# A hybrid decoder layer on one core: another order and engine choice for the first stage, loads by single blocks, five weight places in turn

## The chip, the core and the metric

The kernel is one program on one core of a Trainium2 chip. The metric is the time of one execution on the device in microseconds (us), less being better. Three runs of the kernel before took 858.31, 863.84 and 863.96 us; their median is 863.84 us.

## The reference

One layer on x of 512 tokens by 1024 channels, all in float32:

```python
h = x @ w_in[l]                                     # one projection feeds everything
y_a = nsa_attention(nsa_q, cmp_k, ..., nsa_gate) @ w_nsa_out[l]      # 8 heads of 64, 3 branches
y_b = gated_deltanet(gdn_qkv, beta, decay, gate) @ w_gdn_out[l]      # 4 heads of 128, chunks of 64
mix = (sigmoid(gate_a) * y_a + sigmoid(gate_b) * y_b) @ w_o[l]
x = layer_norm(ALPHA * x + mix, ln1_g[l], ln1_b[l])
f = conv_ffn(x, ffn_w_up[l], ffn_conv_w[l], ffn_w_down[l])           # 1024 -> 2 x 2816 -> 1024
x = layer_norm(ALPHA * x + f, ln2_g[l], ln2_b[l])
```

In each DeltaNet head a unit lower triangular system of 64 by 64 is solved in each chunk (`solve_triangular(eye + m, eye)`); the attention has a compressed, a selected and a window branch.

## The kernel before

**Products.** Every float32 product is made of three products of rounded halves: a = hi + lo, and hi·hi + lo·hi + hi·lo are added up in PSUM. So each weight block is loaded (`raw`), rounded by ACT (`wh`, L216) and its rest taken by DVE or POOL (`wl`, L220, or L1043 in the last stage), before TensorE (PE) can use it. `split_w` does this in the first stage; which engine takes a step is looked up in the table `ENGINE` (A, V and G are ACT, DVE and POOL), with names such as `ws13` for the `wl` of unit 13, `wh13` for its `wh`, and `sq1` for the last step of q in head 1.

**Stages** (times of the profiled execution): a start in which the token-major columns are made for all tokens at once (`token_major`, L270 to L292, tiles `pb`; 5 to 19 us); the first stage up to 366 us, in which the projection's other columns are made unit by unit (`gemm_t`, tiles `gps`, L230 to L233), the four DeltaNet heads are worked off and the attention's blocks of scores are made (L777, L778), normalised, transposed (L806) and multiplied with the values (L823); the merge and the output projection until 500 us; the FFN's first product (tiles `pu`) until 741 us; the FFN's second product (L1107) until 852 us; the last normalisation.

**What sets the order.** In the first stage each step has a short name: q0 is the convolution of head 0, n0 the triangular solve of head 0 (`gdn_tri`, L490 to L564), o0 its output, a0 to a7 and b0 to b7 the attention's heads, and so on. `ORDER` lists the steps, `SHIFT` moves one in the planner's eyes by some units of time, and a scheduler that is given the priorities writes out one order of instructions for each engine. Each engine then works its own list strictly in that order, and waits at an instruction until its inputs are there. DMAs of inputs are issued from SyncE's (SP's) list in the same manner, and a tile's place in a pool (`BUFS` gives how many) has to come free before it is loaded again.

**The triangular solve.** For head h, POOL or DVE makes `lo` (L494) and `gx` (L502), PE spreads them (L504), ACT copies them (L505), and DVE works off 30 small steps in a row, `tmp = lx * xs` (L511) and `xs = xs + tmp` (L512). The result is spread to `z` (L514), and only then PE can transpose it (L402, `dps<-ident,z`) and go on in short dependent products.

**The FFN's second product.** It is made as seven products of half matrices (`go`, L1121). `go` works through groups of two weight blocks (`block`, L1027 to L1045); the first of a group takes one of three places (`wh`, `wl`), the second one of two (`wh2`, `wl2`). The two halves of the tokens (t = 0 and 1) have a PSUM bank each (`px`, `pz`, `pu`). After the last group of a product DVE takes the banks into x (L1137, L1141). The sums of activations for later products are split in between (`sum_parts`, hs on ACT, sl on DVE, L1102).

Of the kernel before, what the change touches and what calls it, by code (L numbers as in the profile page):

```python
# [2 lines left out]

# [125 lines left out]


@with_exitstack
def body(ctx: ExitStack, tc: tile.TileContext, d, out):
# [136 lines left out]

    def token_major():  # L270
        pss = [pb.tile([128, 288], F32, name=f"pb{t}") for t in range(TT)]
        for k0 in range(0, KD, 2):
            load_x(k0)
            hi, lo = split_w(d["wB"][:, k0:k0 + 2, :], [128, 2, 288], V)
            load_x(k0 + 1)
            for i in range(2):
# [2 lines left out]
                for t in range(TT):
                    ts = slice(t * 128, (t + 1) * 128)  # L280
                    PE.matmul(pss[t], xh[:, k, ts], wh, start=(k == 0), stop=False)
                    PE.matmul(pss[t], xh[:, k, ts], wl, start=False, stop=False)
                    PE.matmul(pss[t], xl[:, k, ts], wh, start=False, stop=(k == KD - 1))
# [936 lines left out]
```

## Time and profile before

| what | value |
|---|---|
| runs, median | 863.84 us (858.31 to 863.96) |
| the profiled execution, its span | 861.92 us, 860.1 us |
| PE busy | 832.0 us (97%), 4226 matmuls |
| DVE busy | 598.1 us (70%) |
| ACT busy | 404.9 us (47%) |
| POOL busy | 171.2 us (20%) |
| DMA | 108.05 MB, 126 GB/s in the mean |

An engine's busy time is the sum of the time in which it had an instruction under way. For PE this says less than it seems: matmuls are pipelined, and one that runs at half the clock is as busy as one at the full clock. So the places where PE waits, and the clock it was granted, have to be read beside it.

### The profile page before, as it was taken

Reading aid. Unit: us, or ns where it says so; the run is one execution under the profiler, and the core shown is the slowest. Engines: PE = TensorE matmul, PEld = TensorE weight load, DVE = VectorE, ACT = ScalarE, POOL = GpSimd, SP = SyncE. Lnnn points to the kernel's source line nnn. Section 1 sums busy time; section 2 is a strip of 40 time slices with the busy share of each in tenths; the row PEclk is TensorE's granted clock in tenths of the full one; section 3 lists DMA queues with packets and bytes.
Section 4 is the critical chain, followed back from the end, with each engine's and each line's share of the span. In section 5 each row is a group of like instructions: output and inputs, shape, how many; then the busy total and the mean of one; then the engine's idle time right before and its main releaser. Section 6 shows DMA issues by size and latency. Waiting matters only on the chain.

```text
span 860.1 us, 11841 instructions
## 1 busy us (share of the span) xinstructions
PE 832.0 (97%) x4226; PEld 685.1 (80%) x4226; DVE 598.1 (70%) x1257; ACT 404.9 (47%) x891; POOL 171.2 (20%) x160
## 2 busy tenths in 40 slices
PE   9999799999899999999999999999999999999996
PEld 8777687778777778888888898888888888887774
DVE  5666479976656876484557637777777777867686
ACT  5553277476356766542234104444444444654541
POOL 0423531414425311202100002111111111100000
PEclk9999799999999999999999999999999999999999
DMA  8323111002011100254347006998875832565562
GB/s 263 109 73 123 37 39 50 26 25 72 27 50 50 41 34 25 74 172 147 123 147 245 24 2 224 277 243 270 189 230 155 221 95 76 173 208 178 180 230 98
DMA packets 35051, 108.05 MB, mean 126 GB/s; under 512 B 3632, under 2 KB 4016, under 8 KB 34608
## 3 DMA queue, kind: packets, MB, share of 16 engines
q1 hardware_dynamic: 27696, 84.23, 30.3%
q0 software_dynamic: 7296, 23.07, 11.3%
q8 instruction: 33, 0.54, 0.3%
q14 instruction: 26, 0.21, 0.1%
HBM read 105.19 MB, written 25.17 MB: 152 GB/s over the span
## 4 chain that ended last, share of the span: by engine, by line
PE 53%; DVE 6%; DMA 5%; issue 1%; ACT 1%; POOL 1%; DVEq 0%; ACTq 0%; POOLq 0%
PE pu L232 9%; PE pu L230 9%; PE pu L233 9%; PE gps L232 3%; PE gps L233 3%; PE gps L230 3%; DMA raw<-wsum 3%; DVE wl L1043 2%; DMA raw<-in_down 2%; PE pw L986 2%; PE pw L984 2%; PE pm L230 2%; PE pw L985 2%; PE pm L232 2%; PE pm L233 2%
## 5 line engine op out<-in xcount | busy, mean ns | idle before, releaser
L220 DVE TENSOR_TENSOR wl<-raw,wh 128x512 fp32r<-128x512 f32 (+1 forms) x142 | 112.2, 791 | 79.7 <-ACT wh L216 66.3
L216 ACT ACTIVATE wh<-raw 128x512 fp32r<-128x512 f32 (+1 forms) x152 | 93.7, 620 | 146.9 <-PE pu L232 100.8
L230 PE MATMUL pu<-mh,wh 128*128 128x512 f32 (+1 forms) x384 | 142.7, 372 | 0.0
L232 PE MATMUL pu<-ml,wh 128*128 128x512 f32 (+1 forms) x384 | 142.6, 371 | 0.0
L233 PE MATMUL pu<-mh,wl 128*128 128x512 f32 (+1 forms) x384 | 142.6, 371 | 0.0
L230 PE MATMUL gps<-xh,wh 128*128 128x512 f32 x320 | 128.9, 404 | 1.4 <-DVE tmp L511 0.8
L232 PE MATMUL gps<-xl,wh 128*128 128x512 f32 x320 | 128.6, 402 | 0.0
L233 PE MATMUL gps<-xh,wl 128*128 128x512 f32 x320 | 128.4, 402 | 0.0
L230 PEld LDWEIGHTS pu<-mh,wh 128*128 128x128 f32 x384 | 72.4, 188 | 12.6
L233 PEld LDWEIGHTS pu<-mh,wl 128*128 128x128 f32 x384 | 72.4, 188 | 12.4
L232 PEld LDWEIGHTS pu<-ml,wh 128*128 128x128 f32 x384 | 72.4, 188 | 12.4
L220 POOL TENSOR_TENSOR wl<-raw,wh 128x512 fp32r<-128x512 f32 x42 | 55.5, 1323 | 134.0 <-ACT wh L216 59.0
L1065 DVE SCALAR_TENSOR_TENSOR fa<-pu,fcw,fa 128x511 f32<-128x511 f32 x88 | 65.7, 746 | 10.8 <-ACT fa L1062 9.2
L230 PEld LDWEIGHTS gps<-xh,wh 128*128 128x128 f32 x320 | 60.6, 190 | 12.8 <-issue 2.2
L232 PEld LDWEIGHTS gps<-xl,wh 128*128 128x128 f32 x320 | 60.6, 190 | 11.3 <-issue 0.7
L233 PEld LDWEIGHTS gps<-xh,wl 128*128 128x128 f32 x320 | 60.6, 190 | 10.5
L1071 POOL TENSOR_TENSOR fth<-fth,fa 128x512 f32<-128x512 f32 x22 | 28.7, 1304 | 201.5 <-DVE fa L1065 201.5
L1042 ACT ACTIVATE wh<-raw 128x512 fp32r<-128x512 f32 x67 | 39.6, 625 | 44.1 <-DMA raw<-wsum 17.5
L1043 DVE TENSOR_TENSOR wl<-raw,wh 128x512 fp32r<-128x512 f32 x67 | 44.9, 701 | 21.9 <-ACT wh L1042 21.7
L263 POOL TENSOR_TENSOR rs<-rs,minus_half 128x1 f32<-128x1 f32 x8 | 7.6, 946 | 184.1 <-DVE rs L945 184.1
L783 ACT ACTIVATE sc<-sc,mn 128x384 f32<-128x384 f32 (+2 forms) x64 | 35.8, 560 | 15.6 <-DVE mn L781 14.9
L1062 ACT ACTIVATE fa<-pu,fcw 128x512 f32<-128x512 f32 x44 | 29.6, 672 | 10.2 <-PE pu L233 10.2
(328 smaller groups left out, 1685.4 us busy)
## 6 DMA issues: line engine op xcount, KB each, us to landing
raw<-in_up SPq DMA_DIRECT2D x44, 512.0 KB, 4.8
raw<-in_wT SPq DMA_DIRECT2D x40, 512.0 KB, 3.5
wsum<-in_down POOLq DMA_DIRECT2D x6, 2816.0 KB, 24.4
raw<-wsum SPq DMA_DIRECT2D x20, 512.0 KB, 4.3
raw<-in_down SPq DMA_DIRECT2D x15, 512.0 KB, 4.0
wsum<-wsum POOLq DMA_DIRECT2D x2, 2816.0 KB, 12.2
raw<-in_wm SPq DMA_DIRECT2D x8, 512.0 KB, 3.7
raw<-in_wo SPq DMA_DIRECT2D x8, 512.0 KB, 3.8
```

The lines of the kernel that those rows point to most:

```text
L216: A.activation(wh, r, AF.Copy)
L220: eng.tensor_tensor(wl, r, wh.bitcast(F32), op=OP.subtract)
L230: i = PE.matmul(ps, wh[k], mh_(k), start=(k == 0), stop=False)
L232: PE.matmul(ps, wh[k], ml_(k), start=False, stop=False)
L233: PE.matmul(ps, wl[k], mh_(k), start=False, stop=(k == n - 1))
L783: A.activation(s[:, i, :n], s[:, i, :n], AF.Exp, scale=-1.0, bias=mn[:, 0, i:i + 1], accum_out=mn[:, 1, i:i + 1])
L984: PE.matmul(ps, mh[:, k, ts], woh[:, k, cs], start=(k == 0), stop=False)
L1042: A.activation(hi, raw[:, i], AF.Copy)
L1043: V.tensor_tensor(lo, raw[:, i], hi.bitcast(F32), op=OP.subtract)
L1062: A.activation(acc, ps, AF.Copy, scale=w[:, 2:3])
L1065: V.scalar_tensor_tensor(acc[:, n:], ps[:, :S - n], w[:, i:i + 1], acc[:, n:], op0=OP.mult, op1=OP.add)
L1071: G.tensor_tensor(th, th, g[1], op=OP.mult)
```

## The change

It has four parts, none of which changes what is computed.

1. Other tables `ORDER`, `SHIFT` and `ENGINE`, so that the first stage's steps stand in another order and some of them on other engines.
2. `load_x` becomes `load_block(k)`: x and the token-major weights `wB` are loaded one block k at a time (before: wB in pairs of blocks); x's first two blocks come in two halves of tokens; the `wh` of block 0 is made by DVE.
3. The pool `mid` has 3 places where it had 4, `out` 4 where it had 3.
4. In the FFN's second product the five places are taken in turn by the blocks, whichever group they are in, and a group works block by block (both token halves of a block, then the next block). Only the last group of a product that has `then` works token half by token half, as all did before.

PE issues the same matmuls in number and form. Over the whole program DVE issues 10 more `wl` of 128x512 (201 to 211), 3 more casts, 2 more steps `kq` and `vraw`, one more tap of the convolution, 2 more `gx` of 128x256, one more `z`, 5 more steps L791, one `lo` less and 3 fewer steps L794 (29 to 26); POOL 10 fewer `wl` (42 to 32), 2 fewer `th` and 2 fewer `kq` or `vraw`, one fewer tap, `gx` 2 fewer, one fewer `z`, one more `lo`, 8 more casts (12 to 20). SP issues 8 loads of wB where it issued 4, and 10 of x where it issued 8.

```diff
@@ tables (SHIFT and ENGINE are left out)
...
-ORDER = "q0 k0 i0 q1 j0 m0 c n0 i1 p0 j1 v0 v1 o0 a0 b0 y0 a1 m1 n1 i2 j2 b1 a2 o1 b2 y1 m2 v2 q2 a3 n2 b3 o2 y2 q3 g0 p1 k1 a4 i3 b4 j3 m3 a5 n3 b5 g1 v3 a6 g2 b6 o3 a7 g3 g4 b7 g5 y3".split()
+ORDER = "q0 k0 i0 q1 j0 m0 c n0 i1 j1 v0 v1 p0 o0 a0 b0 y0 a1 m1 b1 a2 n1 i2 j2 b2 o1 y1 m2 v2 a3 n2 q2 b3 o2 y2 q3 g0 p1 k1 i3 j3 a4 b4 m3 a5 n3 g1 g2 b5 a6 v3 g3 b6 a7 g4 b7 o3 g5 y3".split()
...
-BUFS = {"w2": 2, 'in': 3, 'st': 6, 'mid': 4, 'out': 3, 'att': 4, 'ob': 1, 'qf': 2, 'kq': 2, 'lx': 1, 'pg': 2, 'pd': 2, 'pa': 3, 'raw': 3, 'wh': 3, 'wl': 3, 'q2': 4, 'mg': 6, 'mr': 4}
+BUFS = {"w2": 2, 'in': 3, 'st': 6, 'mid': 3, 'out': 4, 'att': 4, 'ob': 1, 'qf': 2, 'kq': 2, 'lx': 1, 'pg': 2, 'pd': 2, 'pa': 3, 'raw': 3, 'wh': 3, 'wl': 3, 'q2': 4, 'mg': 6, 'mr': 4}
@@ the token-major start
-    def load_x(k):
+    def load_block(k):
+
         xr = slot("mid", "xr")
-        nc.sync.dma_start(out=xr, in_=d["xT"][:, k, :])
-        A.activation(xh[:, k, :], xr, AF.Copy)
-        V.tensor_tensor(xl[:, k, :], xr, xh[:, k, :].bitcast(F32), op=OP.subtract)
+        raw = wp.tile([128, 288], F32, name="raw", bufs=BUFS["raw"])
+        wh = wp.tile([128, 288], F32R, name="wh", bufs=BUFS["wh"])
+        wl = wp.tile([128, 288], F32R, name="wl", bufs=BUFS["wl"])
+        n = 2 if k < 2 else 1
+        halves = [slice(i * S // n, (i + 1) * S // n) for i in range(n)]
+        for i, ts in enumerate(halves):
+            nc.sync.dma_start(out=xr[:, ts], in_=d["xT"][:, k, ts])
+            if i == 0:
+                nc.sync.dma_start(out=raw, in_=d["wB"][:, k, :])
+            A.activation(xh[:, k, ts], xr[:, ts], AF.Copy)
+            if i == 0:
+                if k == 0:
+                    V.tensor_copy(wh, raw)
+                else:
+                    A.activation(wh, raw, AF.Copy)
+                V.tensor_tensor(wl, raw, wh.bitcast(F32), op=OP.subtract)
+            V.tensor_tensor(xl[:, k, ts], xr[:, ts], xh[:, k, ts].bitcast(F32), op=OP.subtract)
+        return wh, wl
...
-        for k0 in range(0, KD, 2):
-            load_x(k0)
-            hi, lo = split_w(d["wB"][:, k0:k0 + 2, :], [128, 2, 288], V)
-            load_x(k0 + 1)
-            for i in range(2):
-                k = k0 + i
-                wh, wl = hi[i], lo[i]
...
+        for k in range(KD):
+            wh, wl = load_block(k)
...
@@ the FFN's second product
+    turn = itertools.cycle(range(5))
...
-            elif i:
+            elif next(turn) > 2:
                 hi = fp.tile([128, S], F32R, name="wh2", bufs=BUFS["w2"])
                 lo = fp.tile([128, S], F32R, name="wl2", bufs=BUFS["w2"])
...
-            for t in range(2):
-                for j, w in zip(js, ws):
-                    three(ps[t], a, j, t, w, fresh and j == 0, j == NP - 1)
+            pairs = [(j, w, t) for j, w in zip(js, ws) for t in range(2)]
+            if then is not None and g == len(GROUPS) - 1:
+                pairs.sort(key=lambda x: x[2])
+            for j, w, t in pairs:
+                three(ps[t], a, j, t, w, fresh and j == 0, j == NP - 1)
```

**The start, SP's list.** Rows are line, DMA, tile and shape. Before, the first weight block of the first stage (`wT`) is issued ahead of the constants:

```order
L202 DMA xr<-in_xT 128x512
L209 DMA raw<-in_wT 128x1024
L302 DMA cst<-in_consts 128x1444
L305 DMA ident<-in_consts 128x128
L312 DMA gcw<-in_gcw 128x48
```

Now, behind the constants:

```order
L210 DMA xr<-in_xT 128x512
L314 DMA cst<-in_consts 128x1444
L226 DMA raw<-in_wT 128x1024
L317 DMA ident<-in_consts 128x128
L324 DMA gcw<-in_gcw 128x48
```

The 722 KB of constants now stand ahead of the first `wT`. On PE the first products of the first stage (`gps`), which stood between the last token-major ones, now all come after them.

**Head 0's solve, POOL's list** while DVE works off the 30 steps. Before (`th` and `kq` are the last steps of head 1's q):

```order
L220 TENSOR_TENSOR wl_1171<-raw_1167,wh_1169 128x512
L220 TENSOR_TENSOR wl_1175<-raw_1167,wh_1173 128x512
L395 TENSOR_TENSOR th_1091<-th_1091,acc_1086 128x512
L396 TENSOR_TENSOR kq_950<-th_1091,acc_1086 128x4x128
L507 COPY xs_2330<-cst_305 128x64
```

Now:

```order
L237 TENSOR_TENSOR wl_1096<-raw_1088,wh_1094 128x512
L237 TENSOR_TENSOR wl_1148<-raw_1144,wh_1146 128x512
L237 TENSOR_TENSOR wl_1152<-raw_1144,wh_1150 128x512
L519 COPY xs_2298<-cst_319 128x64
L237 TENSOR_TENSOR wl_1409<-raw_1405,wh_1407 128x512
```

The two steps are one step of DVE now, and stand there behind `z`. PE's products between L504 and the transposes of `z` are 49 of 128x512 before and now.

**Head 2's solve, PE's list** up to the transposes of `z`. `cs` is the compressed branch's probabilities. Before:

```order
L232 MATMUL gps_2747<-xl_94,wh_2743 128x512
L233 MATMUL gps_2747<-xh_93,wl_2745 128x512
L402 MATMUL aps_2728<-ident_307,cs_2713 128x128 x4
L402 MATMUL dps_2365<-ident_307,z_2363 128x128 x4
L523 MATMUL dps_2372<-z_2363,m_2131 128x64 x4
```

Now:

```order
L250 MATMUL gps_2584<-xh_93,wl_2582 128x512
L247 MATMUL gps_2584<-xh_93,wh_2580 128x512
L414 MATMUL dps_2333<-ident_321,z_2331 128x128 x4
L535 MATMUL dps_2340<-z_2331,m_2144 128x64 x4
L414 MATMUL aps_2742<-ident_321,cs_2727 128x128
```

The transposes of `cs` moved behind those of `z`, and between L504 and `z` there are 46 products of 128x512 where there were 37.

## Rows read from the trace of the kernel before

**Rows 1.** The page: the engines' busy us, share of the span, instructions.

```profile
PE 832.0 (97%) x4226; PEld 685.1 (80%) x4226; DVE 598.1 (70%) x1257; ACT 404.9 (47%) x891; POOL 171.2 (20%) x160
```

**Rows 2.** Windows: length, busy PE, PEld, DVE, ACT, POOL, clock, DMA share, GB/s.

```profile
140.00:179.00 39.00, 36.99 (x198) 28.65 (x196) 37.55 (x120) 22.01 (x56) 12.46 (x12) 1.00 0.13 41
...
283.00:305.00 22.00, 20.48 (x110) 15.71 (x109) 20.66 (x72) 15.24 (x38) 4.41 (x5) 1.00 0.13 44
...
740.00:860.00 120.00, 109.05 (x468) 86.40 (x466) 89.16 (x140) 55.03 (x89) 5.40 (x5) 0.98 0.56 182
```

**Rows 3.** The same view of shorter windows.

```profile
80.00:100.00 20.00, 15.62 (x65) 13.03 (x64) 13.84 (x35) 5.37 (x9) 9.16 (x8) 0.79 0.18 53
...
175.00:200.00 25.00, 24.02 (x176) 19.70 (x175) 18.61 (x67) 20.66 (x68) 5.97 (x7) 0.93 0.06 15
225.00:250.00 25.00, 22.38 (x150) 18.32 (x149) 17.95 (x51) 11.90 (x28) 6.65 (x7) 0.93 0.15 44
```

**Rows 4.** PE's waits: who waited for whom, us in total, times, longest.

```profile
PE dps L402 <- DVE z L514: 3.6, 1, 3.6
PE aps L402 <- DVE xs L512: 1.7, 1, 1.7
PE px L1107 <- DVE wl L1043: 1.5, 2, 1.0
...
PE pz L1107 <- DVE wl L1043: 0.9, 2, 0.7
...
PE pb L281 <- ACT wh L216: 0.5, 1, 0.5
```

**Rows 5.** Timeline of DVE in head 0's solve: start, duration, instruction.

```profile
80.91 0.21 DVE L512 TENSOR_TENSOR xs<-xs,tmp 128x52 f32<-128x52 f32 x1
81.16 1.21 DVE L511 TENSOR_TENSOR tmp<-lx,xs 128x48 f32<-128x48 f32 x1
...
90.17 1.14 DVE L512 TENSOR_TENSOR xs<-xs,tmp 128x8 f32<-128x8 f32 x1
```

**Rows 6.** Timeline of POOL beside it.

```profile
81.00 1.30 POOL L220 TENSOR_TENSOR wl<-raw,wh 128x512 fp32r<-128x512 f32 x1 [4.23 <-ACT wh L216]
...
90.02 1.27 POOL L395 TENSOR_TENSOR th<-th,acc 128x512 f32<-128x512 f32 x1 [2.28 <-ACT th L391]
91.36 1.27 POOL L396 TENSOR_TENSOR kq<-th,acc 128x512 f32<-128x512 f32 x1
```

**Rows 7.** Timeline of PE behind head 0's solve.

```profile
93.44 1.12 PE L402 MATMUL dps<-ident,z 128*128 128x128 f32 x4 [3.60 <-DVE z L514]
...
96.48 0.63 PE L233 MATMUL gps<-xh,wl 128*128 128x512 f32 x1
...
102.21 0.40 PE L233 MATMUL gps<-xh,wl 128*128 128x512 f32 x1
102.45 0.40 PE L230 MATMUL gps<-xh,wh 128*128 128x512 f32 x1
```

**Rows 8.** Groups by line up to 366 us: busy us, mean ns.

```profile
L220 POOL TENSOR_TENSOR wl<-raw,wh 128x512 fp32r<-128x512 f32 x38 | 49.3, 1299 | 92.3 <-ACT wh L216 59.0 <-DVE wh L218 13.2 <-PE gps L233 11.3
...
L220 DVE TENSOR_TENSOR wl<-raw,wh 128x512 fp32r<-128x512 f32 x27 | 19.1, 706 | 18.3 <-POOL wh L218 8.8 <-ACT wh L216 7.3 <-PE aps L692 1.6
```

**Rows 9.** DMAs issued before 16 us: KB each, median us to landing.

```profile
raw<-in_wT SPq DMA_DIRECT2D x2, 512.0 KB, 6.6
cst<-in_consts SPq DMA_DIRECT2D x1, 722.0 KB, 7.9
```

**Rows 10.** Timeline of SP and of PE in the start.

```profile
11.06 0.42 SPq L302 DMA_DIRECT2D cst<-in_consts  x1
...
18.13 0.39 PE L230 MATMUL gps<-xh,wh 128*128 128x512 f32 x1
```

**Rows 11.** Timeline of PE and DVE where a weight block comes late.

```profile
806.15 2.35 DVE L1102 TENSOR_TENSOR sl<-sr,hs 128x1024 fp32r<-128x1024 f32 x2
...
809.16 0.50 PE L1107 MATMUL pz<-wl,hs 128*128 128x512 f32 x1 [0.70 <-DVE wl L1043]
```

More of the change, by code (lines that the diff above doesn't have):

```diff
@@ L1 @@
+import itertools
 import math
@@ L123 @@
 LAG = 1
-SHIFT = {'q0': -80, 'a0': -2606, 'b0': -1465, 'a1': -346, 'b1': -377, 'a2': -230, 'q3': -2244, 'j3': -430, 'a4': -1433, 'g2': 1384, 'o2': -123, 'i1': -141, 'b5': -1403, 'y2': 203, 'q1': -513, 'g1': -578, 'y3': 2104, 'y1': -290, 'b3': -285, 'k0': -80, 'm2': 160, 'g3': 1052, 'b6': 744, 'v2': 140, 'j1': -94, 'm0': 33, 'b7': -911, 'o3': -214, 'y0': 12, 'q2': -38, 'g4': 84, 'm3': -270, 'v0': -40, 'j0': -160, 'v1': -14, 'o1': -84, 'v3': -40, 'o0': 67, 'n2': -1041, 'g0': -210, 'b2': -127, 'k1': -309, 'j2': 199, 'p0': 131, 'a3': -41, 'm1': -225, 'n3': -4, 'n1': -883, 'i0': 12, 'a5': -2, 'p1': -12, 'i2': -88, 'i3': -21, 'n0': -6, 'a6': 155}
@@ L125 @@
-ENGINE = {'p16': 'A', 'p55': 'V', 'p24': 'G', 'p32': 'A', 'vb0': 'A', 'p43': 'A', 'p04': 'G', 'p54': 'A', 'p20': 'G', 'kd2': 'A', 'p25': 'A', 'kd0': 'V', 'p06': 'A', 'vb1': 'A', 'lo3': 'G', 'p44': 'A', 'p45': 'G', 'p34': 'G', 'p36': 'A', 'kd1': 'A', 'kd3': 'A', 'sq1': 'G', 'xs3': 'G', 'vb2': 'A', 'wh31': 'V', 'ws4': 'G', 'ws11': 'V', 'ws29': 'G', 'p03': 'A', 'wh2': 'A', 'wh43': 'G', 'p37': 'A', 'ws43': 'V', 'wh42': 'G', 'ws30': 'G', 'wh8': 'V', 'ws14': 'V', 'wh32': 'A', 'wh35': 'G', 'ws15': 'V', 'sq3': 'G', 'y1': 'G', 'z3': 'G', 'wh0': 'A', 'wh36': 'V', 'wh38': 'V', 'wh1': 'G', 'ws1': 'V', 'ws18': 'V', 'ws38': 'V', 'p26': 'V', 'wh39': 'V', 'sv2': 'V', 'sk0': 'V', 'p33': 'A', 'ws16': 'V', 'ws36': 'V', 'ws40': 'V', 'ws5': 'V', 'p47': 'A', 'xs2': 'G', 'ck2': 'G', 'wh34': 'G', 'ws21': 'G', 'wh46': 'G', 'ws42': 'V', 'wh47': 'G', 'ws32': 'V', 'wh44': 'V', 'ws34': 'V', 'ws39': 'V', 'lo0': 'V', 'gx80': 'G', 'gx81': 'G', 'gx82': 'G', 'gx83': 'V', 'xs1': 'G', 'ws27': 'G', 'sv0': 'G', 'ws0': 'V', 'wh5': 'G', 'wh22': 'G', 'ws9': 'V', 'wh6': 'A', 'wh17': 'V', 'cv1': 'V', 'wh37': 'V', 'ws25': 'V', 'ws17': 'V', 'ws20': 'V', 'wh14': 'G', 'wh30': 'V', 'cv2': 'G', 'wh33': 'V', 'ws28': 'V', 'cv21': 'G', 'ws35': 'V', 'wh24': 'V', 'ck0': 'G', 'y2': 'G', 'p46': 'G', 'ck1': 'G', 'ck30': 'G', 'p07': 'G', 'p56': 'G', 'y3': 'A', 'z2': 'G'}
@@ L126 @@
-ORDER = "q0 k0 i0 q1 j0 m0 c n0 i1 p0 j1 v0 v1 o0 a0 b0 y0 a1 m1 n1 i2 j2 b1 a2 o1 b2 y1 m2 v2 q2 a3 n2 b3 o2 y2 q3 g0 p1 k1 a4 i3 b4 j3 m3 a5 n3 b5 g1 v3 a6 g2 b6 o3 a7 g3 g4 b7 g5 y3".split()
+SHIFT = {'q0': -132, 'a0': -2225, 'b0': -1907, 'a1': -1387, 'b1': -413, 'a2': -168, 'q3': -2520, 'j3': -1367, 'a4': -2212, 'g2': 3031, 'o2': -1958, 'i1': -141, 'b5': -1016, 'y2': 152, 'q1': -3760, 'g1': -1660, 'y3': 4851, 'y1': 94, 'b3': -598, 'k0': -54, 'm2': -122, 'g3': 1542, 'b6': 259, 'v2': 240, 'j1': -111, 'm0': -1466, 'b7': -3021, 'o3': 1031, 'y0': 163, 'q2': 2544, 'g4': -378, 'm3': -748, 'v0': -140, 'j0': -1735, 'v1': 51, 'o1': -2858, 'v3': 253, 'o0': -57, 'n2': -541, 'g0': -111, 'b2': -100, 'k1': -84, 'j2': 191, 'p0': 151, 'a3': 105, 'm1': -561, 'n3': 206, 'n1': -576, 'i0': 60, 'a5': -49, 'p1': -58, 'i2': -126, 'i3': 23, 'n0': 35, 'a6': 241, 'g5': 132, 'b4': -10, 'a7': 930}
@@ new lines @@
+ENGINE = {'p16': 'A', 'p55': 'G', 'p24': 'A', 'p32': 'A', 'vb0': 'A', 'p43': 'A', 'p04': 'G', 'p54': 'A', 'p20': 'G', 'kd2': 'A', 'p25': 'A', 'kd0': 'V', 'p06': 'A', 'vb1': 'A', 'lo3': 'G', 'p44': 'A', 'p45': 'V', 'p34': 'G', 'p36': 'A', 'kd1': 'A', 'kd3': 'A', 'sq1': 'V', 'xs3': 'G', 'vb2': 'A', 'wh31': 'V', 'ws4': 'V', 'ws11': 'V', 'ws29': 'V', 'p03': 'V', 'wh2': 'A', 'wh43': 'G', 'p37': 'A', 'ws43': 'V', 'wh42': 'G', 'ws30': 'V', 'wh8': 'V', 'ws14': 'G', 'wh32': 'G', 'wh35': 'A', 'ws15': 'G', 'sq3': 'V', 'y1': 'G', 'z3': 'V', 'wh0': 'G', 'wh36': 'V', 'wh38': 'G', 'wh1': 'V', 'ws1': 'V', 'ws18': 'V', 'ws38': 'G', 'p26': 'V', 'wh39': 'G', 'sv2': 'V', 'sk0': 'V', 'p33': 'V', 'ws16': 'V', 'ws36': 'G', 'ws40': 'V', 'ws5': 'V', 'p47': 'A', 'xs2': 'G', 'ck2': 'V', 'wh34': 'G', 'ws21': 'G', 'wh46': 'G', 'ws42': 'V', 'wh47': 'G', 'ws32': 'V', 'wh44': 'V', 'ws34': 'G', 'ws39': 'V', 'lo0': 'G', 'gx80': 'V', 'gx81': 'G', 'gx82': 'V', 'gx83': 'V', 'xs1': 'G', 'ws27': 'G', 'sv0': 'V', 'ws0': 'V', 'wh5': 'V', 'wh22': 'A', 'ws9': 'V', 'wh6': 'A', 'wh17': 'A', 'cv1': 'V', 'wh37': 'A', 'ws25': 'G', 'ws17': 'V', 'ws20': 'V', 'wh14': 'V', 'wh30': 'A', 'cv2': 'G', 'wh33': 'G', 'ws28': 'V', 'cv21': 'G', 'ws35': 'V', 'wh24': 'V', 'ck0': 'G', 'y2': 'A', 'p46': 'A', 'ck1': 'G', 'ck30': 'V', 'p07': 'V', 'p56': 'G', 'y3': 'G', 'z2': 'G', 'ws13': 'G', 'ws12': 'V', 'ws31': 'V', 'p57': 'A', 'gx160': 'V', 'wh13': 'G', 'p17': 'G', 'wh4': 'A', 'ws19': 'V', 'sk3': 'G', 'wh21': 'G', 'wh28': 'G', 'wh15': 'G', 'ws37': 'V', 'p22': 'A', 'ws33': 'V', 'wh16': 'A', 'ws24': 'V', 'ck31': 'V', 'vb3': 'V', 'xs0': 'G', 'wh3': 'A', 'ws10': 'V', 'wh12': 'A', 'ws23': 'G', 'p05': 'A', 'wh11': 'V', 'ws26': 'V', 'wh25': 'V', 'wh26': 'V', 'cq32': 'V', 'p23': 'G', 'cv11': 'G', 'wh19': 'V'}
@@ L271, in token_major @@
         pss = [pb.tile([128, 288], F32, name=f"pb{t}") for t in range(TT)]
-        for k0 in range(0, KD, 2):
-            load_x(k0)
-            hi, lo = split_w(d["wB"][:, k0:k0 + 2, :], [128, 2, 288], V)
-            load_x(k0 + 1)
-            for i in range(2):
-                k = k0 + i
-                wh, wl = hi[i], lo[i]
[L279 to L283, printed above, removed]
+        for k in range(KD):
+            wh, wl = load_block(k)
+            for t in range(TT):
+                ts = slice(t * 128, (t + 1) * 128)
+                PE.matmul(pss[t], xh[:, k, ts], wh, start=(k == 0), stop=False)
+                PE.matmul(pss[t], xh[:, k, ts], wl, start=False, stop=False)
+                PE.matmul(pss[t], xl[:, k, ts], wh, start=False, stop=(k == KD - 1))
         for t in range(TT):
```

## The prediction

> **What bounds the kernel.** I first read the busy times: PE is busy for 832.0 us, 97% of the span [rows 1], and the change takes no matmul away and adds none. So time can only come from where PE waits, from where its clock is low, or from a wait that is added. Busy time hides the second: a 128x512 matmul takes 0.63 us at 96.48 and 0.40 us at 102.45 [rows 7], both counted as busy. Next I read windows by stage. The granted clock is 1.00 nearly everywhere, with three dips: 0.79 in 80 to 100 us, 0.93 in 175 to 200 and in 225 to 250 [rows 3]. The dips lie where the triangular solves of heads 0, 1 and 2 end. Last I read PE's waits: the longest is 3.6 us for `z` of head 0, then 1.7 us behind the solve of head 2; in the FFN's second product 1.5 and 0.9 us for `wl`; 0.5 us in the start [rows 4]. DVE, which is 70% busy over the whole span, is full in two stretches, 37.55 of 39 us from 140 and 20.66 of 22 us from 283 [rows 2]. PE is the bound, then, and DVE sets when it waits in the first stage.
>
> The profiled execution took 861.92 us, its span and 1.8 us around it; the median of the three runs, 863.84, is 1.92 us above it. The sum is made against 861.9.
>
> **Why the solve of head 0 is late.** One of its steps takes 0.21 us, and the next, just as small, 1.21 us [rows 5]. The long one begins at 81.16 and ends at 82.37, where POOL's `wl` runs from 81.00 to 82.30 [rows 6]: DVE stood still until POOL was done. The same is seen at 90.17, beside `th` from 90.02 [rows 5, 6]; `kq`, from 91.36, follows. So one POOL instruction with two inputs costs such a chain about 1.21 − 0.21 = 1.0 us.
>
> **The change, part by part.**
>
> *Head 0.* `th` and `kq` of head 1's q leave POOL and become one DVE step behind `z`. The four `wl` on POOL stay. Two stretched steps less are 2 × 1.0 us; I take −1.9 us, since the step at 90.17 was stretched by 0.95 only. PE's cover for the solve is 49 products before and now, so the wait of 3.6 us becomes about 1.7 us. Ends: nothing (other POOL work slides in) and −3.6. What is late next is head 1's q, one step later on DVE, wanted only in the next solve.
>
> *The clock behind it.* The window of 80 to 100 us has 0.79 [rows 3]: 20 × 0.21 = 4.2 us of full-speed time lost, idle included. PE fell after the wait of 3.60 us, among short dependent products [rows 7]. With half of that wait gone I take about a third back, −1.5 us; ends 0 and −4.2.
>
> *Heads 1 and 2.* Either dip costs 25 × 0.07 = 1.75 us [rows 3]. In head 2 the transposes of `cs`, where PE waited 1.7 us [rows 4], move behind those of `z`, and nine more 128x512 products stand ahead of `z`. Such products start 0.24 us apart at the full clock (102.21 and 102.45 [rows 7]), so nine are 2.2 us of cover, against 1.7 us of wait and three more steps of DVE. I take −1.2 us of wait (0 to −1.7), and for the two dips together −1.5 us of clock (0 to −3.5). Head 1's solve gets some score products in its tail; I count it in the clock.
>
> *The start.* The first products wait 0.5 us for `wh` [rows 4]; with half of x's first block and one block of weights to wait for, that can go: −0.5 at best. Against it: the first stage's own first weights are now issued behind the 722 KB of constants, not ahead. The constants are issued at 11.06 and take 7.9 us, to 18.96, when 512 KB of `wT` stand ahead of them [rows 9, 10]. Both together end at about the same time in either order, so `wT` lands near 19.2, and with one rounding step of some 0.7 us (the `wl` of that size takes 0.706 [rows 8]) its first product stands near 19.9, where it was 18.13 [rows 10]. Before, it was mixed with the last few token-major products, of which I take half a us to have been left, so PE lost nothing: those alone would have ended near 18.6, and now end near 18.1. PE then idles for about 1.8 us. Net 19.9 − 18.6 = +1.3 us; ends −0.5 (the constants don't delay it) and +3 (three places in `mid` hold up the loads too). The six added loads I cost at nothing else: the two DMAs of rows 9 were under way beside each other, and what is loaded stays the same.
>
> *DVE's load.* In the first stage DVE gets ten `wl` at 0.706 us, 7.1 us, and POOL loses them at 1.299 [rows 8]. The other steps that DVE gets (casts, `kq`, `vraw`, a tap, two `gx`, a `z`, less a `lo`) are near 5 us by the same rate of 0.4 to 0.7 us each: 12 us in all. Most of it lies beside PE, as DVE has room outside the two full stretches. These are 61 us of the roughly 330 in which the steps are spread, so 12 × 61/330 = 2.2 us would fall where there is no room. Against that POOL has 17 fewer two-input instructions, each of which could hold DVE up by 1.0 us [rows 5]. I take +1.5; ends 0 and +12.
>
> The Trainium skill (SBUF — State Buffer, "SBUF: two separate sides") says that such a meeting is a lock held for the whole instruction, and that the loser, either engine, blocks fully. The row of 1.21 us agrees for DVE. By the lock alone, the 17 instructions taken off POOL give DVE back up to 17 us where it gets 12; spread as above, (12 − 17) × 61/330 is −0.9, the term is −0.9 instead of +1.5, and the time 854.2. I give that 0.15 of the forecast's chance.
>
> *The FFN's second product.* PE waits 1.5 + 0.9 us for `wl` here [rows 4]; the window's clock is 0.98 [rows 2], most of it the end. At 809.16 `wl` came late because DVE had two `sl` of 2.35 us in hand [rows 11]. With five places in turn every block can be made two and a half groups ahead; before, the second of a group had two places only. And working block by block frees a place half a group, some 1.4 us, earlier and asks for the second block 0.7 us later. The waits seen are 1.0 us at most each, so I take −2.0; ends 0 (DVE itself is late) and −2.4. The takes at the end of a product now stand side by side on DVE; queued behind them are `wl` that can be a little later, which the places cover.
>
> *Edits with no term.* `mid` 3 and `out` 4: a fourth `mid` tile in a solve would wait for a reader that is long done, except in the start, where it is counted.
>
> **Sum:** −1.9 (head 0) − 1.5 (its clock) − 1.2 − 1.5 (heads 1 and 2) + 1.3 (start) + 1.5 (DVE) − 2.0 (FFN) = −5.3, from 861.9 to **856.6 us**. Against the median that is 0.8% less.
>
> **The rivals.**
>
> *A. The waits and dips go altogether.* For it: they hang together, since PE's clock fell only behind such waits. 3.6 + 4.2 + 1.7 + 3.5 + 2.4 = 15.4 us less, with +1.3 in the start 847.8 us. Against it: the four `wl` on POOL still stretch head 0's chain. Chance 0.2.
>
> *B. DVE becomes the bound, and the kernel is slower.* The place is 140 to 179 and 283 to 305 us, where DVE has 1.45 and 1.34 us to spare [rows 2]. If the table heaps its added 12 us there, or on steps for which PE waits, each us is a us of PE. From about 5 us on the path it eats up the gains; all of it without gains is 861.9 + 12 = 874 us, 1.2% over the median. For it: ten `wl` moved on to the engine that is full. Against it: POOL's instructions no longer hold it up. Chance 0.13.
>
> *C. The waits just move.* Another order has other steps on DVE in the solves; a hole closed in head 0 opens in head 1 or 3, and PE ends where it did: 862 us. For it: each solve is a chain of 30 dependent steps in any order. Chance 0.24.
>
> **How the numbers follow.** The forecast has 0.43; with its terms off by half of what lies to their nearer ends it lies in 852 to 860. The range of 8 in 10 takes in most of A and C and the near part of B: **847 to 868**. A measurement of this kernel can tell about 1% from no change, so the bounds are 855.2 and 872.5. Faster: all of A, 0.2, and 0.17 of the forecast (the 0.15 above among it): 0.37. Slower: the far part of B, 0.1, and no other. Same: the rest, 0.53. The predicted time is the forecast's, 856.6.
>
> **What would show it.** In the changed profile: PE's wait for `z` in head 0 near 1.7 us, and DVE's small steps stretched in four places, not six; the clock of the stretch behind it above 0.79, or not; no wait for `xs` ahead of the transposes of `cs`; a gap of 1 to 3 us on PE between the last token-major product and the first of the first stage, with `wT` landing behind the constants; waits for `wl` in the FFN's second product under 1 us in sum. The prediction is wrong if PE's time up to 366 us changes by more than 8 us either way, if the FFN's second product takes as long as before, or if new waits for DVE appear in 140 to 180 or 280 to 305 us.

## The result and the profile after

The changed kernel takes 853.32 us (median of 15 runs, 850.04 to 857.83) where the kernel before took 863.47 us in the runs beside it (15 runs, 857.00 to 870.46): a ratio of 0.9891, 95% interval 0.9869 to 0.9913; by that ratio it is 9.4 us less (7.5 to 11.3). The prediction was 856.6 us, with 847 to 868 as its range.

The profiled execution shows only half of that: 856.81 us where the one of before took 861.92, a span of 855.0 us in place of 860.1. Both halves have to be explained. The table shows when PE came to the same points of the program in five profiles (us from the span's start; "again" is a second profile of the changed kernel, and "start_only" has the change's start alone, both from the experiments below).

| PE's first instruction of | before | after | again | start_only | q1_pool |
|---|---|---|---|---|---|
| first stage's own products | 18.13 | 23.10 | 20.54 | 20.33 | 21.29 |
| z of head 0 | 93.44 | 96.23 | 94.25 | 96.19 | 95.15 |
| z of head 1 | 179.04 | 181.93 | 179.05 | 181.75 | 178.21 |
| z of head 2 | 234.37 | 234.22 | 231.38 | 237.08 | 230.55 |
| z of head 3 | 312.41 | 308.37 | 305.51 | 315.10 | 304.76 |
| merge | 365.94 | 361.19 | 358.30 | 368.59 | 357.32 |
| FFN's second product | 741.11 | 736.28 | 733.59 | 743.38 | 732.37 |
| PE's last instruction | 851.80 | 846.75 | 845.60 | 854.97 | 841.34 |

From before to after: +5.0 us up to the first product, −2.2 up to head 0's z, +0.1 up to head 1's, −3.0 up to head 2's (55.33 to 52.29), −3.9 up to head 3's (78.04 to 74.15), −0.7 up to the merge, −0.1 up to the FFN's second product, −0.2 in it. The two middle steps are the steady part. In eight profiles with the new tables they take 52.3 and 74.1 to 74.2 us: after, again, mid4, pair_mid4, old_ffn, q1_pool (one entry of a table taken back), and tables_only and old_start, which have the old start. In the three with the old tables (before, ffn_only, start_only) they take 55.3 to 55.4 and 78.0. So these 6.9 us come from the tables, whatever the start and the FFN's form. (Three kernels further down, with other tables again, are far slower.)

What the first stage gained is seen in two numbers as well. From its first product to the merge (18.13 to 365.94 before, 23.10 to 361.19 after) PE is idle for 15.6 us before (347.81 less 332.25 busy) and for 7.5 us after (338.09 less 330.55); in again, q1_pool, mid4 and old_ffn it is 7.9 to 8.2 us. And its clock is at half speed (1.2 in place of 2.4 GHz) for 17.1 us of it before, 13.7 after, 10.2 in again. Taking half of such a stretch as lost, an estimate, 8.1 us of idle time and 1.7 us of clock make up the 9.7 us of the profile after.

The page after, where [rows 1] stood:

```profile
PE 830.5 (97%) x4226; PEld 683.5 (80%) x4226; DVE 598.1 (70%) x1278; ACT 401.6 (47%) x886; POOL 155.2 (18%) x150
```

DVE has 21 instructions more and is busy for the same 598.1 us. POOL lost 16.0 us.

Windows after, columns as in [rows 2, 3]:

```profile
140.00:179.00 39.00, 38.06 (x205) 30.05 (x205) 36.88 (x120) 24.75 (x63) 9.51 (x8) 1.00 0.13 42
...
283.00:305.00 22.00, 21.89 (x125) 17.52 (x124) 19.96 (x73) 16.71 (x40) 4.33 (x5) 1.00 0.09 25
```

```profile
80.00:100.00 20.00, 17.15 (x72) 13.86 (x72) 15.45 (x42) 8.42 (x19) 8.01 (x7) 0.87 0.21 69
100.00:125.00 25.00, 24.53 (x162) 19.59 (x161) 14.10 (x36) 13.62 (x49) 9.45 (x8) 0.90 0.15 43
175.00:200.00 25.00, 23.77 (x177) 18.38 (x175) 21.49 (x78) 18.75 (x64) 6.39 (x8) 1.00 0.14 43
225.00:250.00 25.00, 23.94 (x177) 19.66 (x177) 19.67 (x57) 12.31 (x30) 5.64 (x6) 1.00 0.14 44
```

The dips behind heads 1 and 2 are gone (0.93 before, 1.00 now). Where DVE was full PE now fills 38.06 of 39 and 21.89 of 22 us (36.99 and 20.48 before). The dip behind head 0 is still there, later: 0.87 in 80 to 100 and 0.90 in 100 to 125 (before 0.79 [rows 3] and 0.96).

The window of before that [rows 3] leaves out:

```profile
100.00:125.00 25.00, 25.00 (x176) 19.98 (x174) 15.08 (x42) 15.76 (x57) 10.69 (x9) 0.96 0.15 44
```

PE's waits after, columns as in [rows 4]:

```profile
PE gps L247 <- DVE acc L400: 2.8, 1, 2.8
PE gps L247 <- ACT wh L233: 2.3, 1, 2.3
PE px L1120 <- ACT w L1055: 1.6, 1, 1.6
PE pu L1120 <- DVE wl L1056: 1.3, 1, 1.3
PE px L1120 <- DVE wl L1056: 1.1, 1, 1.1
PE dps L414 <- POOL z L526: 1.1, 1, 1.1
```

The waits of 3.6 and 1.7 us of [rows 4] are gone, and new ones stand there: for the convolution's taps (`acc`), for the first weights in the start (`wh`), and in the FFN's second product.

### The profile page after: what moved, and what is told of

It is laid out like the page before. It is cut to its first block, busy times and chain, and to the rows that moved or that the text cites. A ratio compares the mean times of both kernels' runs of the same rounds, so it can differ in the third digit from the quotient of the medians.

```text
span 855.0 us, 11887 instructions
## 1 busy us (share of the span) xinstructions
PE 830.5 (97%) x4226; PEld 683.5 (80%) x4226; DVE 598.1 (70%) x1278; ACT 401.6 (47%) x886; POOL 155.2 (18%) x150
## 3 DMA queue, kind: packets, MB, share of 16 engines
q0 software_dynamic: 7296, 23.07, 11.5%
## 4 chain that ended last, share of the span: by engine, by line
PE 52%; DVE 5%; DMA 5%; ACT 1%; issue 1%; POOL 0%; DVEq 0%; ACTq 0%; POOLq 0%
PE pu L249 9%; PE pu L247 9%; PE pu L250 9%; PE gps L247 3%; PE gps L249 3%; PE gps L250 3%; DVE wl L1056 3%; DMA raw<-wsum 3%; DMA raw<-in_down 2%; PE pw L996 2%; PE pw L998 2%; PE pw L997 2%; PE pm L249 2%; PE pm L247 2%; PE pm L250 2%
## 5 line engine op out<-in xcount | busy, mean ns | idle before, releaser
L237 DVE TENSOR_TENSOR wl<-raw,wh 128x512 fp32r<-128x512 f32 x144 | 117.9, 822 | 69.8 <-ACT wh L233 61.5
L233 ACT ACTIVATE wh<-raw 128x512 fp32r<-128x512 f32 x134 | 84.3, 630 | 151.5 <-PE pu L249 102.4
L249 PEld LDWEIGHTS pu<-ml,wh 128*128 128x128 f32 x384 | 72.3, 188 | 12.3
L1055 ACT ACTIVATE wh<-raw 128x512 fp32r<-128x512 f32 x67 | 40.6, 627 | 39.3 <-DMA raw<-wsum 12.4
L237 POOL TENSOR_TENSOR wl<-raw,wh 128x512 fp32r<-128x512 f32 x32 | 41.4, 1296 | 91.1 <-ACT wh L233 33.2
L1056 DVE TENSOR_TENSOR wl<-raw,wh 128x512 fp32r<-128x512 f32 x67 | 43.6, 684 | 20.4 <-ACT wh L1055 20.3
L795 ACT ACTIVATE sc<-sc,mn 128x384 f32<-128x384 f32 (+2 forms) x64 | 35.8, 560 | 12.8 <-DVE mn L793 9.0
L1075 ACT ACTIVATE fa<-pu,fcw 128x512 f32<-128x512 f32 x44 | 29.6, 672 | 10.2 <-PE pu L250 10.2
```

Of the source, the lines that this page charges most:

```text
L233: A.activation(wh, r, AF.Copy)
L237: eng.tensor_tensor(wl, r, wh.bitcast(F32), op=OP.subtract)
L249: PE.matmul(ps, wh[k], ml_(k), start=False, stop=False)
L795: A.activation(s[:, i, :n], s[:, i, :n], AF.Exp, scale=-1.0, bias=mn[:, 0, i:i + 1], accum_out=mn[:, 1, i:i + 1])
L1075: A.activation(acc, ps, AF.Copy, scale=w[:, 2:3])
```

## The experiments

Ratios are to runs of the kernel before on the same chip, with the 95% interval; times are medians.

**The parts alone.** Three kernels have one part of the change each, with the places in `mid` and `out` as before, and a fourth all but the start and those places.

```diff
# ffn_only: kernel before, with
...
+            elif next(turn) > 2:
...
+            pairs = [(j, w, t) for j, w in zip(js, ws) for t in range(2)]
...
# start_only: kernel before, with load_block in token_major
# tables_only: kernel before, with the new ORDER, SHIFT and ENGINE
# old_start: changed kernel, with load_x by pairs and
+BUFS = {... 'mid': 4, 'out': 3, ...}
```

> The kernel before with the FFN part of the change alone (five places in turn, block by block). Theory 1 (from the changed kernel's profile, where the FFN's second product takes 110.5 us against 110.7): waits for weights only move inside it, and the time stays within 1.5 us of the kernel before's 863.5. Rival (the prediction's term): the places were what PE waited for, and 2.0 us go, 861.5, with PE's waits in the second product below 1 us in sum.

> The kernel before with the start by single blocks alone (its tables and its four mid places kept). Theory 1: single blocks take 8 raw places one after the other, the first weights of the first stage get their place late and stand behind the constants, so the first product of the first stage begins at 22 to 23 us where it began at 18.1; 3.5 to 5 us slower, 867 to 868.5. Rival: the tables made the start late, not the single blocks; first product before 19.5 us and time within 1 us of 863.5.

> The kernel before with the new ORDER, SHIFT and ENGINE alone (start, places and FFN as before). Theory 1: all of the gain is the tables', and the start gives 4 to 5 us of it back; so this is faster than the whole change: 848 to 850, 13 to 15 us under the kernel before. Rival: the late start only fills time that head 0's solve would have waited anyway, and the tables alone give what the whole change gives, 852 to 854.

> The changed kernel with the old start (x by whole blocks, wB in pairs) and the old numbers of places (mid 4, out 3). Theory 1: 4 to 5 us faster than the changed kernel's 853.3, so 848 to 850; first product of the first stage before 19.5 us and no low clock there. Rival: head 0's solve waits longer instead, and it stays within 1.5 us of 853.3.

| kernel | us | ratio | interval | against before |
|---|---|---|---|---|
| ffn_only | 859.97 | 0.9985 | 0.9969 to 1.0001 | −1.3 |
| start_only | 865.04 | 1.0043 | 1.0024 to 1.0063 | +3.7 |
| tables_only | 856.49 | 0.9948 | 0.9930 to 0.9967 | −4.5 |
| old_start | 856.53 | 0.9948 | 0.9928 to 0.9968 | −4.5 |

The start alone costs about what theory 1 said (3.5 to 5 us), though its first product begins at 20.33 us and not at 22 to 23. But the other two runs refute it: with the old start the new tables give less than with the new one, not more. Their rivals' numbers (852 to 854, and within 1.5 us of 853.3) don't hold either. The parts add up to −2.1 us, the whole is −9.4. The difference arises in the first part of the first stage: PE comes to head 1's z at 179.04 us before, at 181.75 in start_only, at 182.60 in tables_only, and at 179.05 in again, which has both. The reason stands in PE's waits of tables_only up to 45 us:

```profile
PE dps L370 <- issue: 2.9, 1, 2.9
PE gps L230 <- ACT wh L216: 1.7, 1, 1.7
```

and in its window behind that:

```profile
30.00:45.00 15.00, 12.11 (x47) 9.82 (x46) 10.87 (x38) 3.79 (x8) 5.95 (x7) 0.83 0.15 44
```

The new tables give the first stage's first products a priority that, with loads by pairs, sets 24 of them ahead of the last token-major ones. The last of these then begins at 26.6 us (19.2 before, 20.5 after), the decays that need them (`dps`, L370) come late, PE waits 2.9 us, and its clock falls. The tables fit the start that they were changed with.

**The start, and the changed kernel once more.** again is the changed kernel itself. mid4 gives `mid` four places and `out` three; pair_mid4 also loads wB in pairs, with x still by single blocks.

```diff
# mid4 and pair_mid4
-'mid': 3, 'out': 4
+'mid': 4, 'out': 3
# pair_mid4, in load_block
+        if k % 2 == 0:
+            raw2 = wp.tile([128, 2, 288], F32, name="raw", bufs=BUFS["raw"])
+            PAIR[0] = raw2
+        raw = PAIR[0][:, k % 2]
...
```

> The changed kernel once more, beside the kernels below. Its first profile had a granted clock of 0.989 and 856.8 us, while nine of its fifteen runs lay at 0.993 to 0.996 and 850.0 to 854.0. Theory 1: the two groups differ by the low clock around head 0's solve alone, which this kernel has in some executions and the kernel before in nearly all; runs at 0.993 or more are 4 to 5 us faster than those at 0.989 to 0.991, and the median stays 9 to 11 us under the kernel before. Rival: the median of before was the odd one; here the change gives 5 us, as the two profiles say.

> The changed kernel with four places in mid and three in out, as before; all else as changed. Theory 1: three places hold back x's last blocks (in the changed profile the last one was issued at 11.70 and landed at 17.79; with four places and the same start, 10.88 and 14.67), so the first product of the first stage begins 2 to 3 us earlier than 23.1, and the time falls by 1.5 to 3 us against the changed kernel beside it. Rival: the constants and the first weights land at the same time anyhow, and nothing changes (within 1 us).

> The changed kernel with mid 4 and out 3, x by single blocks as changed, but wB loaded in pairs of blocks again, so that the token-major loads take 4 raw places and not 8, and the first weights of the first stage are issued ahead of the constants. Theory 1: the first product of the first stage begins before 19.5 us and the time is 3 to 5 us below the changed kernel beside it. Rival: as with the old start, PE's order then has products of the first stage ahead of the last token-major ones, these end near 26 us, the decays come late, and the time is within 1.5 us of the changed kernel or above it.

again: 851.80 us, ratio 0.9889 (0.9865 to 0.9913). So the gain is 9.6 us and not the 5 us of two profiles. Its runs show why. The two at a granted clock of 0.991 and 0.993 took 855.67 and 852.39 us, the four at 0.994 to 0.996 took 849.29 to 851.95; of the first fifteen runs the six at 0.989 to 0.991 took 853.56 to 857.83, the nine at 0.993 to 0.996 took 850.04 to 854.01. The profile after is one of those six. The kernel before lay at 0.980 to 0.990 in 44 of the 50 runs beside the experiments, and at 0.992 or 0.993 in six. At the same granted clock the two kernels are 4 to 6 us apart: at 0.989 the medians are 860.8 us before (6 runs) and 857.0 after (3), at 0.993 they are 858.1 (5) and 852.6 (2). The other half of the 9.6 us goes with the clock, 0.988 in the mean of the 50 runs and 0.993 in that of the 21. The records of low clock (half speed) agree: 10.2 us behind head 0 and 3.4 us in the first 40 us in the profile after, 6.8 and 3.4 in again, 3.4 and 3.4 in q1_pool, and 10.2 + 3.4 + 3.4 in the kernel before, ffn_only and start_only alike. By estimate each 3.4 us at half speed costs PE up to 1.7 us. That the runs at 0.996 have no dip behind head 0 was not seen in a profile.

mid4: 854.70 us, ratio 0.9918 (0.9894 to 0.9943): not faster, and theory 1 is refuted. In again, with three places, the last token-major product began at 18.8 us, with four at 19.0; the late landing in the profile after was that execution's.

pair_mid4: 854.27 us, ratio 0.9930 (0.9902 to 0.9957). Its first product stands at 17.16 us, as theory 1 said, and yet the rival is right: the last token-major product begins at 24.5, PE waits 2.4 us for the decays, and the clock falls at 38.2.

**Head 0.** In the changed kernel the solve's chain takes 11.50 us from first to last step, in the kernel before 13.58; three steps are stretched, five before. DVE there, after, with POOL and PE beside it:

```profile
85.41 1.18 DVE L523 TENSOR_TENSOR tmp<-lx,xs 128x48 f32<-128x48 f32 x1
...
89.49 1.16 DVE L524 TENSOR_TENSOR xs<-xs,tmp 128x24 f32<-128x24 f32 x1
...
90.91 1.14 DVE L524 TENSOR_TENSOR xs<-xs,tmp 128x20 f32<-128x20 f32 x1
...
93.21 0.74 DVE L400 SCALAR_TENSOR_TENSOR acc<-gps,gcw,acc 128x511 f32<-128x511 f32 x1
93.87 0.15 DVE L523 TENSOR_TENSOR tmp<-lx,xs 128x4 f32<-128x4 f32 x1
93.99 0.75 DVE L400 SCALAR_TENSOR_TENSOR acc<-gps,gcw,acc 128x510 f32<-128x510 f32 x1
94.66 0.16 DVE L524 TENSOR_TENSOR xs<-xs,tmp 128x4 f32<-128x4 f32 x1
94.77 0.75 DVE L400 SCALAR_TENSOR_TENSOR acc<-gps,gcw,acc 128x509 f32<-128x509 f32 x1
95.44 0.68 DVE L526 TENSOR_TENSOR z<-xs,cst 128x512 f32<-128x512 f32 x1
```

```profile
89.26 2.75 POOL L237 TENSOR_TENSOR wl<-raw,wh 128x512 fp32r<-128x512 f32 x2 [2.74 <-ACT wh L233]
```

```profile
95.67 0.77 PE L247 MATMUL gps<-xh,wh 128*128 128x512 f32 x1 [2.85 <-DVE acc L400]
```

`th` and `kq` no longer meet the chain, and the stretched steps are again those beside POOL's `wl`. But three taps of head 1's q (0.75 us each) now stand among the last steps, and PE's next product needs the PSUM bank that they read: PE waits 2.85 us for them, and `z` comes right behind. They are no new work in the chain. Before, the same three stood in it at 86.35, 87.70 and 88.47, and PE waited 0.78 us for their bank there. The first of them, before:

```profile
86.35 0.74 DVE L388 SCALAR_TENSOR_TENSOR acc<-gps,gcw,acc 128x511 f32<-128x511 f32 x1
```

Two experiments went at this: q1_pool puts `th` and `kq` back on POOL, cq1_one takes the first tap off DVE.

```diff
# q1_pool
-'sq1': 'V'
+'sq1': 'G'
# cq1_one
+'cq12': 'G'
```

> The changed kernel with the last step of head 1's q back on POOL (sq1, th and kq, two POOL instructions beside head 0's solve). Theory 1 (the prediction's first term): two of the solve's small steps are stretched by 1.0 us each, and the kernel is 1 to 2.5 us slower than the changed kernel beside it, with the transposes of z in head 0 that much later. Rival: PE waits there for the convolution's taps on DVE and not for the solve, and the time stays within 0.8 us.

> The changed kernel with the first tap of head 1's q on POOL and ACT instead of DVE. In the changed profile the three taps stand among the last steps of head 0's solve, 2.25 us of DVE, and PE waits 2.85 us for them at 95.67. The edit puts the taps behind z, and PE's list has no product ahead of the transposes of z that needs their bank. Theory: head 0's chain to the end of z falls from 12.8 us to about 10.6, with nine products less as cover, which PE does behind z instead; 1 to 2.5 us faster than the changed kernel, 850 to 852. Rival: the cover that is gone and the low clock behind it eat it up, and the time stays within 1 us.

q1_pool: 852.42 us, ratio 0.9899 (0.9880 to 0.9919), 0.6 us above again, within the rival's 0.8. It doesn't test the term: `th` began at 95.09 us there, behind the chain, so that still three steps were stretched. cq1_one: 895.20 us, ratio 1.0393 (1.0371 to 1.0414), 43 us slower than the changed kernel, where all theories said within a few us. The solve up to the end of `z` took 12.3 us (12.8 in the profile after), not 10.6, since POOL's tap met it as well: four stretched steps. So this edit shows the stretching itself, the other way round from the change. With one more POOL instruction beside the chain, one more step is stretched (a step of this size takes 0.20 us in the profile after, at 89.26):

```profile
89.16 1.28 POOL L398 TENSOR_TENSOR acc<-acc,tap 128x511 f32<-128x511 f32 x1
```

```profile
89.28 1.20 DVE L523 TENSOR_TENSOR tmp<-lx,xs 128x24 f32<-128x24 f32 x1
```

That is not where the 43 us went. In the traces, with buffer numbers left out, about 300 of some 3570 lines of PE's list stand elsewhere in cq1_one than in the changed kernel; for q1_pool it is 8, and between the kernels before and after 240. The scheduler works by priority, and one step that is ready at another time can shift much of what follows. What it then did in head 2's solve, PE:

```profile
223.80 0.39 PE L250 MATMUL gps<-xh,wl 128*128 128x512 f32 x1
230.66 0.80 PE L247 MATMUL gps<-xh,wh 128*128 128x512 f32 x1 [6.48 <-ACT qf L673]
231.26 0.63 PE L249 MATMUL gps<-xl,wh 128*128 128x512 f32 x1
```

DVE and ACT:

```profile
226.22 0.69 DVE L237 TENSOR_TENSOR wl<-raw,wh 128x512 fp32r<-128x512 f32 x1
...
227.06 0.68 DVE L672 SCALAR_TENSOR_TENSOR q<-gps,q 64x512 fp32r<-64x512 f32 x1
```

```profile
224.22 0.59 ACT L671 ACTIVATE q<-gps 64x512 fp32r<-64x512 f32 x1 [2.34 <-PE gps L250]
227.77 0.59 ACT L673 ACTIVATE qf<-gps 64x512 f32<-64x512 f32 x1 [2.96 <-DVE q L672]
```

A bank is held by `qf`, which waits for DVE's `q`, which stands among the steps of head 2's chain. PE stands still for 6.48 us, and goes on at half speed (0.63 us for a product of 0.40). The window behind has it for long:

```profile
234.00:283.00 49.00, 45.20 (x244) 35.22 (x243) 24.63 (x55) 18.95 (x51) 6.60 (x7) 0.81 0.10 33
```

This wait is the largest of many. From the first product to the merge PE is idle for 33.9 us in cq1_one (8.2 in again) and at half speed for 41.0 us (10.2 in again); 34.6 of the 43 us are lost behind head 2's z.

**Which table.** old_engine and old_order are the changed kernel with one of the tables taken back.

```diff
# old_engine: the old ENGINE
# old_order: the old ORDER and SHIFT
```

> The changed kernel with the old ENGINE table (the new ORDER and SHIFT, start, places and FFN kept): DVE gets its twelve us of steps back to POOL. In all profiles with the new tables the time from head 1's z to head 2's is 52.3 us (55.3 before), and from head 2's to head 3's 74.2 (78.0 before). Theory 1: the engine choice gives a good part of it, since fewer POOL instructions hold DVE up; with the old table the solves of heads 0 and 2 are stretched again (head 0's from 11.5 to about 13.5 us), and the kernel is 3 to 6 us slower than the changed kernel's 851.8 to 853.3. Rival: the order alone gives it, and the time stays within 1.5 us.

> The changed kernel with the old ORDER and SHIFT (new ENGINE, start, places and FFN kept). Theory 1: the order gives the other part (products moved ahead of head 2's z, transposes of cs behind it): 3 to 6 us slower than the changed kernel, with the wait ahead of the transposes of cs back near 1.7 us. Rival: the engine choice alone gives the gain, and the time stays within 1.5 us of the changed kernel.

old_engine: 894.03 us, ratio 1.0384 (1.0359 to 1.0409). old_order: 880.17 us, ratio 1.0223 (1.0198 to 1.0248). Both are far slower than either whole kernel. In old_engine PE waits 7.1 us for `qf` as in cq1_one, and about 340 lines of its list stand elsewhere; in old_order it is 360, and the waits are many (4.2 us for `z`, 3.2 for `qf`, 3.0 for a step of the scores, 2.5 for the decays). So the gain can't be divided between order and engine choice: neither theory's numbers hold, and neither rival's. What inside the tables gives it stays open.

**The FFN again.** old_ffn is the changed kernel without the FFN part.

```diff
# old_ffn: changed kernel, with
+            elif i:
+            for t in range(2):
+                for j, w in zip(js, ws):
```

> The changed kernel with the FFN's second product as before (two places for the second block of a group, token half by token half). Theory: the FFN part gives about what it gave alone, 1.3 us, so this is 0 to 2.5 us slower than the changed kernel; the wait of 1.3 us near 752 us, behind three sl and two takes on DVE, is gone, and five to eight smaller waits for weights are back. Rival (the prediction): 2 us or more slower.

855.85 us, ratio 0.9939 (0.9919 to 0.9958). Against again's 0.9889 that is 4 us of gain by the FFN part, each with ±2 us and on different chips; alone it gave 1.3 (−0.1 to 2.7). Part of the 4 us is the clock: at 0.993 and 0.994 three runs of old_ffn took 852.93 to 855.30 us and five of the changed kernel 851.64 to 854.01, a difference of 1.6 us between the medians. The profiles say nothing of the kind: the second product took 108.6 to 112.0 us in seven profiles with the new form (ffn_only, old_start, after, again, mid4, pair_mid4, q1_pool) and 108.9 to 112.0 in the four with the old form (before, start_only, tables_only, old_ffn), and PE's waits in it, nearly all for weights, were 2.3 to 4.7 us and 2.2 to 3.5. In cq1_one, old_engine and old_order, with the new form too, it took 110.9 to 114.8 us. What the profiles do show is the new form's own wait, here in the profile after:

```profile
749.04 3.42 DVE L1115 TENSOR_TENSOR sl<-sr,hs 128x768 fp32r<-128x768 f32 x3
752.37 1.28 DVE L1152 SCALAR_TENSOR_TENSOR x<-x,px 128x512 f32<-128x512 f32 x2
753.57 3.69 DVE L1056 TENSOR_TENSOR wl<-raw,wh 128x512 fp32r<-128x512 f32 x6
```

```profile
754.30 0.50 PE L1120 MATMUL pu<-wl,ph 128*128 128x512 f32 x1 [1.31 <-DVE wl L1056]
```

Three `sl` and the two takes stand in a row ahead of six `wl`. This wait of 1.3 to 1.7 us is in every profile with the new form and in none of the old. What the FFN part gives, between nothing and some 4 us, stays open.

## Why the prediction was right, and where not

The forecast's direction and size hold: 9.4 us less measured, 7.2 forecast against the median of before (5.3 against its profile, where the two profiles differ by 5.1). That the profile's sum fits so well is luck. By the table of the result, the start cost 5.0 us (term +1.3), the rest of the first stage gave 9.7 (the other terms up to there make −4.6), and the FFN's second product gave 0.2 (term −2.0). Errors of 3.7, 5.1 and 1.8 us nearly cancel.

- **Head 0, −1.9: the mechanism holds.** Chain 2.08 us shorter, five stretched steps now three. (The prediction counted six and four, and four `wl` on POOL; three stand in the chain before and after.) PE's idle time there fell from 4.4 us (0.78 + 3.60) to 2.85, by 1.5 us and not 1.9, since the taps now end the chain and PE waits for their bank. The term read POOL's list alone, and not where DVE's other steps stand. That a POOL instruction stretches a step of the chain is shown by cq1_one; that `th` and `kq` did so rests on which steps are stretched in the profiles.
- **Its clock, −1.5: not in the profile after.** The low stretch is as long there as before (10.2 us), and shorter in again (6.8) and q1_pool (3.4), by estimate 1.7 and 3.4 us of time. So the term lies in what the runs show, but one execution has it and another not. Two readings behind it were off. The window of 80 to 100 us holds 4.2 of the 5.1 us lost, since 100 to 125 has 0.96. And the clock fell within PE's wait (89.83 to 93.44) and not behind it: it is 1.00 in 91.0 to 91.4 and 0.50 in 91.8 to 92.2 us.
- **Heads 1 and 2, −2.7: right, too small.** −3.0 us up to head 2's z and −3.9 from there to head 3's; the wait of 1.7 us ahead of `cs` and both dips are gone. The low clock behind head 2's z (3.4 us, worth up to 1.7) falls into the second of the two.
- **DVE's load, +1.5: wrong in sign.** Twelve us of steps were added (12.2 by the mean time of each shape before), and DVE is busy for no longer, as the steps of each shape took 11.5 us less in sum. That fewer POOL instructions hold it up would explain that; it is shown for single steps of head 0's chain only. In the two full stretches PE does 1.1 and 1.4 us more, though the work in them is not quite the same, and its waits in 140 to 180 and 280 to 305 us fell from 2.0 and 1.8 us to 1.0 and nothing. Rival B had DVE's load as its price and did not come about. The Trainium skill (SBUF — State Buffer, "SBUF: two separate sides") makes a meeting of a DVE step that reads two inputs from SBUF with a POOL instruction that reads SBUF a lock for the whole instruction. In head 0's chain the trace agrees: steps of about 0.2 us took 1.12 to 1.21 us before and 1.14 to 1.18 after beside POOL's instructions of 1.27 to 1.38 (one of the five before took 0.77). The term by that rule, −0.9, was nearer, and I gave it too little weight.
- **The start, +1.3: right in mechanism, too small.** The constants do stand ahead of the first weights and land first. In the profile after:

```profile
12.08 0.44 SPq L314 DMA_DIRECT2D cst<-in_consts  x1
14.13 0.33 SPq L226 DMA_DIRECT2D raw<-in_wT  x1
```

```profile
22.42 1.15 ACT L233 ACTIVATE wh<-raw 128x512 fp32r<-128x512 f32 x2 [1.98 <-DMA raw<-in_wT]
```

```profile
23.10 0.77 PE L247 MATMUL gps<-xh,wh 128*128 128x512 f32 x1 [2.30 <-ACT wh L233]
```

  The first weights were issued at 14.13 us, since eight single blocks pass through three `raw` places where four pairs did, and not at 10.63; with pairs again (pair_mid4) they were issued at 9.77. I had moved them only behind the constants, not in time. They then took 8.2 us to land, in again 6.1, so part of the 23.10 is that execution's (20.54 in again). Alone the start measured +3.7 us (2.1 to 5.4). Beside the new tables it gains instead: with the old start (old_start) the ratio is 0.9948, with the new one 0.9891. The term had only its cost.
- **The FFN, −2.0: not shown.** The step that failed is "`wl` that can be a little later, which the places cover": they don't, by 1.3 us. PE's waits for `wl` there are 2.4 us in the profile after, where less than 1 was forecast, and the product takes as long as before (110.5 and 110.7 us), which the prediction had named as a sign of being wrong.
- **What no term had:** the parts depend on each other. The sum treated them as independent, and the parts measured alone come to −2.1 us, not −9.4. Each term was read from the final order, in which all parts are in place; that this brought the sum near is argued, not shown.

Rival A named the right source for the second half of the gain, the clock: nine of fifteen runs took 850.0 to 854.0 us, between its 847.8 and the forecast. Its premise, that the clock fell only behind the long waits, doesn't hold for head 1, where it fell at 187.2 us behind waits of 0.46 and 0.36 us. Rival C was right in part on head 0, where the wait moved from `z` to the taps.

## What to carry to other kernels

Read a change to a scheduler's tables from the order that comes out, stretch by stretch, and price the waits there; don't price its parts by taking them back one at a time, since one step that moves can shift everything behind it (43 us for one tap here). When something is taken off a chain, look on every engine of the chain for where its other steps then stand. One profile is one execution: where a low clock comes and goes, look at the clock of many runs before a difference of half a percent is explained.

## What the runs showed of the hardware

The same program ran at 0.991 or at 0.996 of the full clock, 855.7 or 849.3 us, on one chip, and the low stretch behind head 0 was 10.2, 6.8 or 3.4 us long with an unchanged or nearly unchanged order of instructions. An engine that was given 21 more instructions, some 12 us of them by their durations, was not busy any longer (598.1 us). One more POOL instruction beside a chain of small DVE steps stretched one more of them, from 0.20 to 1.20 us. The clock fell within a wait of PE of 3.60 us, and in another place behind waits of 0.46 and 0.36 us.
